# A hybrid attention/Fourier encoder layer: Nyquist weights taken from zero columns of other folds, and the rare rows of both sequences transformed together

## The chip, the cores and the metric

The kernel runs on one core of a Trainium2 chip. One launch computes a whole encoder layer for two sequences. The metric is the device time of a launch in microseconds; the median of the runs of the kernel before is 2137.72 us (2137.21 the lowest). The engines are named as in the profile: PE is TensorE (matmuls), PEld its weight loads, DVE VectorE, ACT ScalarE, POOL GpSimd, SP SyncE, which here issues most DMAs.

## The reference

Each of two sequences is x of 1024 x 1024 in fp32. The layer modulates and normalises it, projects it once, and sends the projection to two branches whose outputs are joined by one output projection; a SwiGLU FFN follows.

```python
def fourier_group(f_in, w_four):                       # f_in: (1, 1024, 512), 8 groups of 64
    f = f_in.reshape(b, s, F_GROUPS, F_GROUP_DIM).astype(jnp.float32)
    fr = jnp.real(jnp.fft.fft2(f, axes=(1, 3), norm='ortho')).astype(f_in.dtype)
    out = jnp.einsum('bsgc,gcd->bsgd', fr, w_four)
    return out.reshape(b, s, FOURIER_WIDTH)

def layer(x, c, ...):
    mod = jax.nn.silu(c) @ w_ada + b_ada
    sh1, sc1, ga1, sh2, sc2, ga2 = ...                 # six vectors of 1024
    h = rmsnorm(x, g_mix) * (1.0 + sc1) + sh1
    z = h @ w_in                                       # q_lat 256, kv_lat 128, k_pe 64, f_in 512
    y_mla = mla_group(q_lat, kv_lat, k_pe, ...)        # latent attention, 4 heads
    y_four = fourier_group(f_in, w_four)
    x = x + ga1 * (concat([y_mla, y_four]) @ w_out)
    h2 = rmsnorm(x, g_ffn) * (1.0 + sc2) + sh2
    return x + ga2 * ((silu(h2 @ w_gate) * (h2 @ w_up)) @ w_down)
```

The change touches the Fourier branch alone: a transform over the 64 channels of each group and over the 1024 positions, its real part, the per-group weights `w_four`, and the Fourier half of `w_out` scaled by `ga1`. Along the channels a real transform of 64 has 33 cosine terms (0 to 32) and 31 sine terms. The last cosine term, number 32, is the Nyquist term. It does not fit into the 32 columns that a group otherwise takes, so the kernel carries it apart: 8 groups give 8 such columns, held three times over (24 columns) for a split product.

## The kernel before, in words

**Arithmetic.** Products in full precision are made of three fast ones: `split` (L59) makes a high part with an ACT copy (L60) and a low part with a DVE subtraction (L61), and `mm3` (L70) adds high*high, high*low and low*high on PE (L71, L72, L73). The three copies of the Nyquist columns do the same inside one product: constant masks (`cmask`) pick high and low parts on both sides, so that one 24-row matmul (L702) stands for three.

**Stage 1, 0 to 246 us.** Eight pairs k = (sequence s, block j of 4) of 2 x 128 rows go through `norm` (L348, two loads of x at L354, a square sum on ACT at L356, the root on POOL in `rstd`, L95 to L102, and a scaling on DVE at L360), `flip` (L363, transposes on PE at L374 and the modulation), `zproj` (L395, the attention part of the projection, with the rotary part at L411 to L415 and the latents' scaling at L416 and L417), `latents` (L425, transposes at L431, stores to `lat_d` at L436), `evenodd` (L381, sums and differences of row halves on POOL at L390) and `fourier_in` (L438, the Fourier part). For pair k the function `pair(k)` (L507) runs the second half of pair k, the flips and even/odd parts of pair k+1 and `norm(k+2)`.

`fourier_in(k, 1)` of the pairs with j == 0 (k = 0 and k = 4) also makes `zo`, a row of the spectrum that needs the odd part of slot 0: 24 matmuls with two columns, one set for each sequence.

Between these steps a generator, `extras` (L266), is advanced three times a pair. It loads modulation weights, folds the value and output weights, and, last, folds `w_four` into `w_out`. That fold runs for two column halves g = 0, 1 (L294 to L318). Each g has four products (p = 0..3, L303) of 128 columns of `lw` with `w_out`, and a fifth group (p == 4, L306) of four matmuls with the 24 Nyquist columns, `lw[:, q, 128:152]`. A product is multiplied by the gate of each sequence on DVE (L310) into a tile `so`, which is stored by two DMAs into `wm_d` (L313); the fifth is stored by one DMA per sequence into `wn_d[s]` (L316). The tiles `so` share a ring of three buffers with other small tiles (`stile`, L168), so a new one waits until the stores of the one three places before have landed.

**Fourier stage, 246 to 350 us.** `zsplit` (L609) splits the spectrum tiles `zc`, `zs` and `zo`; `dft` (L621) does the transform over positions for q = 0, 2, 1, where q == 2 is the 24 Nyquist columns; `prep_wm` (L655) loads and splits the folded weights; `fourier_out` (L691) multiplies both and stores the result to `fo_d`, in the order j = 1, 2, 3, 0 for each sequence and for g = 0, 1. Each (j, g) has six matmuls with A, the Nyquist one (L702), and six with B; an ACT copy and two DVE operations (L127 subtracts, L130 adds) make two output tiles `ed`. For j == 0, output row 512 is added to the row that `ed[1]` holds: `dc_prep` (L676) makes the difference `dl` of two columns of A, six matmuls multiply it, L714 and L715 make two Nyquist rows, and three one-row DVE adds put them together.

**Order of the work.** The program is a plain sequence of calls; a scheduler fixes the order of instructions on each engine when the kernel is built, and engines and SP's DMA issue run in that order. An instruction that waits holds back everything behind it on its engine. Attention and FFN follow from 350 us to the end.

Of the kernel before, what the change touches and what calls it, by code (L numbers as in the profile page):

```python
# [12 lines left out]
F32 = mybir.dt.float32  # L13
# [8 lines left out]
P = 128  # L22
# [22 lines left out]
NCS = NZC + NZS  # L45
NTE = 258
# [4 lines left out]
def hybrid_encoder_kernel(ctx: ExitStack, tc: tile.TileContext, a: dict):  # L51
# [33 lines left out]
    cmask = const.tile([P, 4], F32, name="cmask")  # L85
# [28 lines left out]
    wn_d = [dram.tile([NNYQ, D], F32, name=f"wn_d{s}") for s in range(2)]  # L114
# [39 lines left out]
    zo = [zp.tile([2, NZC], F32, name=f"zo{s}") for s in range(2)]  # L154

    with ExitStack() as st:
# [23 lines left out]
        lw = w.tile([P, 4, 2 * 64 + NNYQ], F32, name="lw")  # L180
# [72 lines left out]
        def small_weights():  # L253
            w4 = w.tile([P, 4, 2, GD], F32, tag="gah0", name="w4")
            nc.sync.dma_start(w4, a["w4"])
            for b in range(2):
# [4 lines left out]
                for p in range(4):  # L261
                    o = P + 2 * p + b
                    nc.vector.tensor_copy(lw[pr, p, o : o + 17 : 8],
                                          w4[pr, p, 0, 32:33].broadcast_to([64, 3]))

        def extras():  # L266
# [27 lines left out]
            for g in range(2):  # L294
# [5 lines left out]
                for p in range(5):  # L300
                    ps = bank()
                    if p < 4:
                        nc.tensor.matmul(ps, lw[:, p, :P], wo4[p // 2][:, p % 2, gs], start=True, stop=True)  # L303
                    else:
                        for q in range(4):
                            nc.tensor.matmul(ps[:NNYQ, :], lw[:, q, P:], wo4[q // 2][:, q % 2, gs], start=(q == 0), stop=(q == 3))  # L306
                    n = P if p < 4 else NNYQ
                    for s in range(2):
                        so = stile("so")
                        nc.vector.tensor_tensor(out=so[:n], in0=ps[:n], in1=ga[s][:n], op=ALU.mult)  # L310
                        if p < 4:
                            for k in range(2):
                                nc.sync.dma_start(wm_d[s][64 * (p % 2) : 64 * (p % 2) + 64, 2 * k + p // 2, gs],  # L313
                                                  so[64 * k : 64 * k + 64, :])
                        else:
                            nc.sync.dma_start(wn_d[s][:, gs], so[:n])  # L316
                    if p % 2 == 1:
                        yield  # L318
# [119 lines left out]
        def fourier_in(k, i):  # L438
# [159 lines left out]
    with ExitStack() as st:  # L598
# [8 lines left out]
        zh, wms = {}, {}  # L607

        def zsplit(s):  # L609
            z = [[wa.tile([P, 4, n], F32R, tag=f"z{k}{i}", name=f"zh{k}{i}", bufs=1) for i in range(2)]  # L610
                 for k, n in enumerate((NZC, NZS))]
            od = [wa.tile([P, NZC], F32R, tag=f"zo{i}", name=f"zod{i}", bufs=1) for i in range(2)]
            for k, src in enumerate((zc[s], zs[s])):
                for c in range(0, 4, 2):
                    split(z[k][0][:, c : c + 2], z[k][1][:, c : c + 2], src[:, c : c + 2])
            for i in range(2):
                nc.vector.tensor_copy(od[i], rd(z[0][i][:, 0, :]))
            split(od[0][0:1, :], od[1][0:1, :], zo[s][0:1, :])
            zh[s] = (z, od)

        def dft(s):  # L621
# [3 lines left out]
            ny = w.tile([NNYQ, NT], F32R, tag="ny", name="ny", bufs=1)  # L625
            for q in (0, 2, 1):
                m = NNYQ if q == 2 else P
                sl = slice(P * q, P * q + m)
                pe, po = bank2(), bank2()
                for c in range(4):  # L630
                    mm3(pe[:m, :NTE], z[0][0][:, c, sl], z[0][1][:, c, sl], tb[0][0][:, c, :NTE], tb[0][1][:, c, :NTE],
                        c == 0, c == 3)
                for c in range(4):
                    zz = [od[i][:, sl] if c == 0 else z[0][i][:, c, sl] for i in range(2)]
# [961 lines left out]
```

## Time and profile before

| what | us |
|---|---|
| median of the runs (lowest) | 2137.72 (2137.21) |
| the profiled execution | 2136.0 |
| its span, first to last instruction | 2134.2 |
| stage 1 | 0 to 246 |
| Fourier stage | 246 to 350 |
| attention and FFN | 350 to 2134 |
| PE busy over the span | 2054.9 |
| granted TensorE clock, mean | 0.989 |

The span is what the profile shows of one execution; the device time is a little longer by what lies around the span. In the rows that are quoted below, a time in front is measured from the span's start. A row of the time line gives start, duration, engine, line, operation, output and inputs, the shape (for a matmul rows*columns of the stationary operand, then the moving one), how many instructions the row joins (x8), and in square brackets how long the engine stood idle before it and what released it. SPq rows are DMA issues of SP. Line numbers are those of the kernel before; in the changed kernel they are up to five lower in stage 1.

### The profile page before, as it was taken

The numbers are of one execution on the slowest core, as the hardware profiler recorded it, in microseconds if no ns is written. First come the engines' busy times: TensorE is split into PE (matmuls) and PEld (weight loads), VectorE is DVE, ScalarE is ACT, GpSimd is POOL, SyncE is SP. The second block draws the span as 40 slices with busy tenths as digits, with TensorE's granted clock in tenths as the row PEclk, the third lists the DMA queues.
The fourth block names the chain that finished last, engine by engine and source line by source line (L and its number), as shares of the span: only waits on it lengthen the run. The fifth ranks groups of instructions, "written<-read, shape, count | busy, mean of one in ns | idle before, by whom it ended". The sixth has DMA issues, their size and how long they took to land. (4 is left out here: it accounts for less than half of the span.)

```text
span 2134.2 us, 28930 instructions
## 1 busy us (share of the span) xinstructions
PE 2054.9 (96%) x10096; PEld 1671.4 (78%) x10096; DVE 1420.7 (67%) x2118; ACT 904.3 (42%) x1758; POOL 826.7 (39%) x1014
## 2 busy tenths in 40 slices
PE   5899998999999998999999999999999999999998
PEld 3787865888888886888888888887788888888876
DVE  2656655766676668786677667777866566557675
ACT  2655522555564546333333336444333333336441
POOL 1455202111222313797797720135545445420142
PEclk8999999999999999999999999999999999999999
DMA  9586656433545355564455468675423222248662
GB/s 366 189 248 181 225 189 234 102 92 92 138 119 124 119 182 203 187 212 168 159 206 188 153 227 290 226 237 175 148 79 119 99 101 97 99 135 290 230 226 101
DMA packets 184387, 371.11 MB, mean 174 GB/s; under 512 B 19280, under 2 KB 58832, under 8 KB 181168
## 3 DMA queue, kind: packets, MB, share of 16 engines
q1 hardware_dynamic: 166384, 313.80, 44.3%
q0 software_dynamic: 17856, 55.45, 8.8%
q8 instruction: 79, 1.29, 0.2%
q14 instruction: 68, 0.56, 0.1%
HBM read 257.18 MB, written 120.39 MB: 177 GB/s over the span
## 5 line engine op out<-in xcount | busy, mean ns | idle before, releaser
L71 PE MATMUL bank<-H,wh 128*128 128x512 f32 x1232 | 489.4, 397 | 13.5 <-DVE val L130 5.0
L73 PE MATMUL bank<-H,wl 128*128 128x512 f32 x1232 | 488.1, 396 | 1.5 <-DVE wl L61 1.5
L72 PE MATMUL bank<-H,wh 128*128 128x512 f32 x1232 | 488.2, 396 | 0.0
L130 DVE TENSOR_TENSOR val<-bank,val 128x512 f32<-128x512 f32 x244 | 167.0, 689 | 191.2 <-PE bank L73 183.4
L71 PEld LDWEIGHTS bank<-H,wh 128*128 128x128 f32 x1232 | 232.2, 188 | 73.2 <-DVE val L130 7.3
L73 PEld LDWEIGHTS bank<-H,wl 128*128 128x128 f32 x1232 | 232.0, 188 | 58.5 <-DVE wl L61 2.3
L72 PEld LDWEIGHTS bank<-H,wh 128*128 128x128 f32 x1232 | 232.0, 188 | 55.8
L61 DVE TENSOR_TENSOR wl<-draw,wh 128x512 fp32r<-128x512 f32 x286 | 200.9, 737 | 80.9 <-ACT wh L60 79.8
L60 ACT CAST wh<-draw 128x512 fp32r<-128x512 f32 x286 | 169.3, 619 | 155.3 <-PE bank L72 76.9
L72 PE MATMUL bank<-wl,wh 128*128 128x512 f32 x572 | 223.7, 391 | 2.2 <-DVE wl L61 2.2
L130 POOL TENSOR_TENSOR val<-val 128x512 f32<-128x512 f32 x58 | 82.8, 1434 | 363.5 <-DVE val L1380 188.6
L73 PE MATMUL bank<-wh,wl 128*128 128x512 f32 x572 | 222.6, 389 | 0.0
L71 PE MATMUL bank<-wh 128*128 128x512 f32 x572 | 222.6, 389 | 0.0
L60 ACT CAST wh<-rgu 128x512 fp32r<-128x512 f32 x172 | 106.7, 621 | 269.4 <-PE bank L72 211.5
L60 ACT CAST wh<-val 128x512 fp32r<-128x512 f32 x133 | 82.2, 621 | 277.6 <-PE bank L72 249.4
L61 DVE TENSOR_TENSOR wl<-val,wh 128x512 fp32r<-128x512 f32 x133 | 139.3, 1049 | 83.5 <-ACT wh L60 83.5
L61 DVE TENSOR_TENSOR wl<-rgu,wh 128x512 fp32r<-128x512 f32 x172 | 167.1, 972 | 4.8 <-ACT wh L60 4.2
L127 POOL TENSOR_TENSOR val<-rgu 128x512 f32<-128x512 f32 x84 | 122.0, 1452 | 120.3 <-DMA rgu<-in_wgu_dram 92.5
L72 PEld LDWEIGHTS bank<-wl,wh 128*128 128x128 f32 x572 | 107.3, 188 | 27.7 <-DVE wl L61 5.7
L71 PEld LDWEIGHTS bank<-wh 128*128 128x128 f32 x572 | 107.4, 188 | 22.3
L73 PEld LDWEIGHTS bank<-wh,wl 128*128 128x128 f32 x572 | 107.4, 188 | 22.1
L127 POOL TENSOR_TENSOR val<-val 128x512 f32<-128x512 f32 x89 | 119.4, 1358 | 1.3
(319 smaller groups left out, 4096.7 us busy)
## 6 DMA issues: line engine op xcount, KB each, us to landing
rgu<-in_wgu_dram SPq DMA_DIRECT2D x86, 512.0 KB, 4.2
draw<-s_d SPq DMA_DIRECT2D x143, 256.0 KB, 4.1
s_d<-val POOLq DMA_DIRECT2D x88, 256.0 KB, 4.1
draw<-t_d SPq DMA_DIRECT2D x88, 256.0 KB, 4.3
s_d<-val SPq DMA_DIRECT2D x66, 256.0 KB, 2.7
draw<-in_w_down_dram SPq DMA_DIRECT2D x55, 256.0 KB, 4.0
wada<-in_w_ada_dram SPq DMA_DIRECT2D x13, 1024.0 KB, 8.8
xt<-in_x_dram SPq DMA_DIRECT2D x16, 512.0 KB, 6.3
```

Source lines behind the costliest of these rows:

```text
L60: here["a"] = nc.scalar.copy(hi, src).ins
L61: here["v"] = nc.vector.tensor_tensor(out=lo, in0=src, in1=rd(hi), op=ALU.subtract).ins
L71: nc.tensor.matmul(out, lh, rh, start=first, stop=False, skip_group_check=cont)
L72: nc.tensor.matmul(out, lh, rl, start=False, stop=False, skip_group_check=cont)
L73: nc.tensor.matmul(out, ll, rh, start=False, stop=last, skip_group_check=cont)
L127: eng.tensor_tensor(out=out, in0=x, in1=y, op=ALU.subtract)
L130: eng.tensor_tensor(out=out, in0=x, in1=y, op=ALU.add)
```

## The change: Nyquist columns in the folds, one transform for both sequences, row 512 directly

Four things are changed.

1. *The fold.* `lw` has 128 columns instead of 152. Its columns 64 and 96 were zero, since the sine terms begin at 1; the Nyquist weights are put there, and the fifth group of matmuls (p == 4) is gone. Rows 64 and 96 of each `so` are then Nyquist rows. A third, small DMA per `so` stores these two rows three times into one `wn_d` of 48 rows for both sequences. `prep_wm` clears these rows in the folded weights with a scaling by a column of `cmask` that is 0 at every 32nd row.
2. *Slot 0.* The rows of both sequences are kept in `zoc`, and one set of 24 matmuls with four columns, in pair 4, replaces the two sets with two columns. A small DMA brings the second sequence's row to partition 0.
3. *The Nyquist transform.* `nyq_split` puts the Nyquist columns of both sequences together; `dft(0)` transforms 48 columns and `dft(1)` leaves q == 2 out. The result `ny` and the weights `wn` are padded with zeros to 128 rows, and the masks pick the sequence.
4. *Row 512.* `dc_prep` is gone. Six matmuls with columns 512:514 of A and one Nyquist matmul accumulate in one bank, and an ACT copy puts the row into `ed[1]`, in place of what stood there.

```diff
-        lw = w.tile([P, 4, 2 * 64 + NNYQ], F32, name="lw")
+        lw = w.tile([P, 4, P], F32, name="lw")
+        zoc = [w.tile([P, NC, ZOW], F32R, name=f"zoc{i}") for i in range(2)]
...
-                for p in range(4):
-                    o = P + 2 * p + b
-                    nc.vector.tensor_copy(lw[pr, p, o : o + 17 : 8],
-                                          w4[pr, p, 0, 32:33].broadcast_to([64, 3]))
+                nc.vector.tensor_copy(lw[pr, :, 64 + 32 * b], w4[pr, :, 0, 32])
...
-                for p in range(5):
+                for p in range(4):
                     ps = bank()
-                    if p < 4:
-                        nc.tensor.matmul(ps, lw[:, p, :P], wo4[p // 2][:, p % 2, gs], start=True, stop=True)
-                    else:
-                        for q in range(4):
-                            nc.tensor.matmul(ps[:NNYQ, :], lw[:, q, P:], wo4[q // 2][:, q % 2, gs], start=(q == 0), stop=(q == 3))
-                    n = P if p < 4 else NNYQ
+                    nc.tensor.matmul(ps, lw[:, p, :], wo4[p // 2][:, p % 2, gs], start=True, stop=True)
                     for s in range(2):
                         so = stile("so")
...
+                        nc.vector.tensor_tensor(out=so, in0=ps, in1=ga[s], op=ALU.mult)
+                        for k in range(2):
+                            nc.sync.dma_start(wm_d[s][64 * (p % 2) : 64 * (p % 2) + 64, 2 * k + p // 2, gs],
+                                              so[64 * k : 64 * k + 64, :])
+                        nc.sync.dma_start(
+                            wn_d[NNYQ * s : NNYQ * s + NNYQ, gs].rearrange("(k r) n -> r k n", k=3)[2 * p : 2 * p + 2],
+                            so[64:97:32, :].unsqueeze(1).broadcast_to([2, 3, 512]))
...
             if i == 1 and j == 0:
+                for k in range(2):
+                    nc.vector.tensor_copy(zoc[k][:, :, 2 * s : 2 * s + 2], rd(eo[1][k][:, :, 0:2]))
+            if i == 1 and j == 0 and s == 1:
                 po = bank()
                 for c in range(NC):
-                    mm3(po[:2, :NZC], eo[1][0][:, c, 0:2], eo[1][1][:, c, 0:2], wcs_h[:, c, :NZC], wcs_l[:, c, :NZC],
+                    mm3(po[:ZOW, :NZC], zoc[0][:, c, :], zoc[1][:, c, :], wcs_h[:, c, :NZC], wcs_l[:, c, :NZC],
                         c == 0, c == NC - 1)
-                nc.vector.tensor_copy(zo[s], po[:2, :NZC])
+                nc.vector.tensor_copy(zo[0], po[:ZOW, :NZC])
+                nc.sync.dma_start(zo[1], zo[0][2:3, :])
...
-            for q in (0, 2, 1):
-                m = NNYQ if q == 2 else P
+            for q in (0, 2, 1) if s == 0 else (0, 1):
+                m = NY2 if q == 2 else P
...
-                    split(wm[0][:, c, gs], wm[1][:, c, gs], raw)
+                    if c < 2:
+                        split(wm[0][:, c, gs], wm[1][:, c, gs], raw)
+                    else:
+                        nc.scalar.activation(wm[0][:, c, gs], raw, AF.Copy, scale=cmask[:, 6:7])
+                        nc.vector.scalar_tensor_tensor(out=wm[1][:, c, gs], in0=raw, scalar=cmask[:, 6:7],
+                                                       in1=rd(wm[0][:, c, gs]), op0=ALU.mult, op1=ALU.subtract)
...
-                wnr = w.tile([NNYQ, 512], F32, tag="wnr", name="wnr", bufs=1)
+                wnr = w.tile([P, 512], F32, tag="wnr", name="wnr", bufs=1)
+                nc.gpsimd.memset(wnr, 0.0)
+                nc.sync.dma_start(wnr[:NY2], wn_d[:, gs])
...
                 if j == 0:
-                    pn = [bank2() for _ in range(3)]
+                    pn = bank2()
                     for q in range(2):
-                        mm3(pn[0][:2, :], dl[0][:, q, :], dl[1][:, q, :], wm[0][:, q, gs], wm[1][:, q, gs], q == 0, q == 1)
-                    nc.tensor.matmul(pn[1][:2, :], ny[:, 512:514], wn[:, gs], start=True, stop=True)
-                    nc.tensor.matmul(pn[2][:2, :], ny[:, 0:2], wn[:, gs], start=True, stop=True)
-                    for q, f in enumerate((add, add, sub)):
-                        f(ed[1][0:1, :], ed[1][0:1, :], pn[q][0:1, :], nc.vector)
+                        mm3(pn[:2, :], A[0][:, q, 512:514], A[1][:, q, 512:514], wm[0][:, q, gs], wm[1][:, q, gs], q == 0, False)
+                    nc.tensor.matmul(pn[:2, :], ny[:, 512:514], wn[:, gs], start=False, stop=True)
+                    nc.scalar.copy(ed[1][0:1, :], pn[0:1, :])
```

More of the change, by code (lines that the diff above doesn't have):

```diff
@@ L45 @@
 NCS = NZC + NZS
+NY2 = 2 * NNYQ
+ZOW = 4
 NTE = 258
@@ L113, in hybrid_encoder_kernel @@
     wm_d = [dram.tile([P, 4, D], F32, name=f"wm_d{s}") for s in range(2)]
-    wn_d = [dram.tile([NNYQ, D], F32, name=f"wn_d{s}") for s in range(2)]
+    wn_d = dram.tile([NY2, D], F32, name="wn_d")
     hc_d = [dram.tile([P, 4, 4, 512], F32, name=f"hc_d{s}") for s in range(2)]
@@ L153, in hybrid_encoder_kernel @@
     zs = [zp.tile([P, 4, NZS], F32, name=f"zs{s}") for s in range(2)]
-    zo = [zp.tile([2, NZC], F32, name=f"zo{s}") for s in range(2)]
+    zo = [zp.tile([ZOW, NZC], F32, name="zo"), zp.tile([1, NZC], F32, name="zo1")]
     with ExitStack() as st:
@@ L644, in dft @@
                     nc.vector.tensor_scalar(out=al, in0=al, scalar1=cmask[:m, 1:2], scalar2=None, op0=ALU.mult)
-                    nc.vector.scalar_tensor_tensor(out=ny, in0=rd(ah), scalar=cmask[:m, 0:1], in1=al,
+                    nc.vector.scalar_tensor_tensor(out=nyt[:m], in0=rd(ah), scalar=cmask[:m, 0:1], in1=al,
                                                    op0=ALU.mult, op1=ALU.add)
@@ L689, in hybrid_encoder_kernel @@
-        dls = {}
         def fourier_out(s, ABn, j):
@@ L1539, in _constants @@
     cmask[8:16, 3] = 1
+    cmask[24:48, 0:2] = cmask[0:24, 0:2]
+    cmask[24:48, 4:6] = cmask[0:24, 2:4]
+    cmask[:, 6] = np.arange(P) % 32 != 0
     r = {
```

78 lines of the change are left out of this document (35 added, 43 removed).

## The prediction

> **What bounds the kernel now.** I read the page's head and busy times first, then a table of stages, then the order of time on single engines inside the two stages that the change touches.
>
> ```profile
> span 2134.2 us, 28930 instructions
> PE 2054.9 (96%) x10096; PEld 1671.4 (78%) x10096; DVE 1420.7 (67%) x2118; ACT 904.3 (42%) x1758; POOL 826.7 (39%) x1014
> 90.00:210.00 120.00, 119.86 (x739) 98.65 (x738) 73.89 (x148) 70.65 (x177) 62.24 (x133) 1.00 0.72 209
> 246.00:350.00 104.00, 101.08 (x504) 67.56 (x505) 67.50 (x146) 35.50 (x76) 0.00 (x0) 1.00 0.70 245
> ```
>
> Columns of the last two: stretch, its length, busy time (instructions) of PE, PEld, DVE, ACT, POOL, granted clock, DMA share, GB/s. PE is the bound: 119.86 of 120 us in most of stage 1, 101 of 104 in the Fourier stage. So PE time taken out counts in full, as long as what stands behind PE's next step in each in-order queue arrives as early as PE does. Attention and FFN, after 350, are not edited and I let them shift as a block.
>
> **PE work that goes.** Rows of PE in order of time: start, duration, line, output and inputs. Matmuls overlap, so I go from start to start.
>
> ```profile
> 85.37 0.29 PE L71 MATMUL bank<-wcs_h,eoh 128*2 128x280 f32 x1
> 88.48 0.36 PE L71 MATMUL bank<-wz_h,hh 128*128 128x448 f32 x1
> 183.86 3.61 PE L306 MATMUL bank<-wada,lw 128*24 128x512 f32 x8
> 187.41 0.47 PE L71 MATMUL bank<-wz_h,hh 128*128 128x448 f32 x1
> 208.49 1.39 PE L374 MATMUL bank<-ident,xt 128*128 128x128 f32 x8
> 209.81 3.61 PE L306 MATMUL bank<-wada,lw 128*24 128x512 f32 x8
> 213.35 0.47 PE L71 MATMUL bank<-wz_h,hh 128*128 128x448 f32 x1
> ```
>
> The 24 two-column slot-0 matmuls of the first sequence take 88.48 - 85.37 = 3.1 us; the second sequence's set stays, with 4 columns. The two Nyquist fold groups (L306) take 3.55 and 3.54. Stage 1 thus loses 10.2 us of PE work.
>
> ```profile
> 284.85 0.40 PE L73 MATMUL bank<-wm,A 128*128 128x512 f32 x1
> 285.18 0.50 PE L702 MATMUL bank<-wn,ny 24*128 24x512 f32 x1
> 285.61 0.50 PE L71 MATMUL bank<-wm,B 128*128 128x512 f32 x1
> 285.95 0.39 PE L72 MATMUL bank<-wm,B 128*128 128x512 f32 x1
> 286.18 0.40 PE L73 MATMUL bank<-wm,B 128*128 128x512 f32 x1
> 294.27 0.38 PE L715 MATMUL bank<-wn,ny 24*2 24x512 f32 x1
> 294.58 0.50 PE L71 MATMUL bank<-wm,A 128*128 128x512 f32 x1
> 304.94 0.28 PE L71 MATMUL bank<-tb,zh 128*24 128x258 f32 x1
> 307.75 0.28 PE L71 MATMUL bank<-tb,zh 128*128 128x258 f32 x1
> ```
>
> The 24-column transform of the second sequence goes: 2.8 us. A 24-row product breaks the stride: neighbours start 0.23 apart (285.95 to 286.18), but around L702 the steps are 0.33, 0.43 and 0.34, 0.40 us lost each, 16 times, 6.4 us in all. The new operands have 128 rows, zero beyond 48. The nearest row with 128 rows keeps 0.23, so I take the whole 0.40; the bounds are 0 and 6.4. In the j==0 step, two 24-row products become one of 128 rows: L715's slot goes (0.31 to the next start, 294.27 to 294.58, of which 0.08 is break), and with the smaller breaks on both sides I count 0.5, four times, 2.0 us.
>
> The Trainium skill, "TensorE: Matmul & The Clock Gate", section "Why this matters for your kernels", says that a lone matmul of few rows takes as long as one of 128; by that the padding would give nothing, 6.4 us less. The rows disagree. "TensorEngine Tiling (Array Packing)", "Key Properties", says that a change of tiling mode drains the engine; that fits the 24 rows, though the 24-column transform (304.94 to 307.75, 24 products at 0.117) shows no such drain.
>
> **End of the Fourier stage.** PE's savings do not all arrive there.
>
> ```profile
> 341.19 0.69 DVE L127 TENSOR_TENSOR ed<-ea,bank 128x512 f32<-128x512 f32 x1 [6.63 <-DMA fo_d<-ed]
> 348.75 1.44 DVE L130 TENSOR_TENSOR ed<-ed,bank 1x512 f32<-1x512 f32 x2
> 350.30 0.68 DVE L127 TENSOR_TENSOR ed<-ed,bank 1x512 f32<-1x512 f32 x1
> 349.47 0.39 PE L71 MATMUL gb<-wq_h,ql 128*128 128x256 f32 x1 [1.29 <-DVE ed L130]
> ```
>
> DVE waits 6.63 us for the stores of `ed` and is then late; PE waits 1.29 for it. Three one-row adds of about 0.67 us per (s, g) go from DVE, replaced by one ACT copy. They cover the last matmuls, so the end follows DVE's 128x512 pairs (two of 0.69 each) instead. In the second output pass PE itself would end 4.2 us earlier (8 x 0.40 + 2 x 0.5); I count 3.1, since DVE's wait for stores stays. The first pass gives 8 x 0.40 + 2 x 0.5 = 4.2, and the transform 2.8. The shared set's 48 columns cost PE nothing (a stride of 0.117 at 24 and at 128 columns), and its small splits, some 0.7 us of DVE, lie beside PE's own waits for the first splits; if not, they cost that 0.7. Fourier: 4.2 + 2.8 + 3.1 = **-10.1 us**, between -3.7 (no stride gain) and -11.2.
>
> **Stage 1: what the change moves.** Rows of SP, which issues DMAs in order, then two lines' answers: issue time in ns and time from issue to landing in us.
>
> ```profile
> 178.42 5.12 SPq L313 DMA_DIRECT2D wm_d<-so  x8
> 183.64 0.53 SPq L354 DMA_DIRECT2D xt<-in_x_dram  x1
> 197.54 5.13 SPq L313 DMA_DIRECT2D wm_d<-so  x8
> 204.12 6.44 SPq L313 DMA_DIRECT2D wm_d<-so  x8
> L316 SPq DMA_DIRECT2D wn_d<-so x4: 300/343/816, 190.2 to 216.4; - x4
> DMA to landing us min/median/max: 4.4/6.3/7.9
> ```
>
> (The last line is that of L354, the x loads.) Before, the second x load of the last pair, norm(7), is issued at 183.64, between the fold groups g=0 and g=1. In the changed program's order on SP it stands behind all of group 1: 24 `so` DMAs (three for each of eight `so`, the third new) and two latent stores. That is the costly edit, and nothing in the diff shows it. Sixteen small DMAs come, four go.
>
> The load waits for the last `so` of group 1. These come in threes of a ring, each needing its old DMAs landed. On DVE the fourth stands behind the even/odd chain of the previous pair:
>
> ```profile
> 198.53 0.60 PE L431 MATMUL bank<-ident,lat 128*128 128x128 f32 x4
> 203.44 2.99 POOL L390 TENSOR_TENSOR eo<-hf 128x512 f32<-128x512 f32 x2 [1.51 <-DVE eol L61]
> 198.58 1.05 ACT L356 ACTIVATE junk<-xt 128x1024 bf16<-128x1024 f32 x1
> 199.82 0.22 POOL L95 TENSOR_SCALAR rs_v<-ms 128x2 f32<-128x2 f32 x1 [0.93 <-ACT junk L356]
> 201.74 0.20 POOL L102 TENSOR_TENSOR rs_r<-rs_w,rs_y 128x2 f32<-128x2 f32 x1
> 203.27 0.75 DVE L360 TENSOR_SCALAR xt<-xt,rs_r 128x1024 f32<-128x1024 f32 x1
> 207.50 0.68 DVE L61 TENSOR_TENSOR eol<-eo,eoh 128x512 fp32r<-128x512 f32 x1
> ```
>
> PE is full, so the first 3.1 us carry to group 0; there the latents of pair 5 (L431) wait for a rope that now stands with the eighth `so`, which I estimate to eat most of them. So fourier_in(5,0), which ended at 198.5, ends 3.55 and a little earlier, at 194.6. The even/odd chain behind it (ACT, DVE, POOL's 2.99, ACT, DVE) took from there to 208.2 before, 9.7; I take 9.0, as DVE has fewer scalings in it now, and it ends at 203.6; the fourth `so` follows at 204. SP then needs, for five `so`, 5 x (2 x 0.64 + 0.34) = 8.1 us (0.64 from 5.12 / 8), and 1.2 for two latent stores: the load is issued at about 213.3. It lands 5.2 later (between the 4.4 and 6.3, since SP goes quiet), 218.5. Then ACT's square 1.2, POOL's chain 2.2 (199.82 to the end of 201.74), two scalings of 0.75 on DVE, the flips 0.8: zproj(6,1) starts at 224.2, where before it was 213.35. **+10.9 us.** PE, through with zproj(6,0) at about 205, has nothing ordered ahead of the flip: an idle of some 15 to 18 us.
>
> Without the chain's delay SP, kept busy from 196 on, needs 16 x 0.64 + 8 x 0.34 + 1.2 and is through at 210.2; with a landing of 4.4 that gives +7.0; with a fourth `so` 1.5 us later and a landing of 7.9, +15.0.
>
> **The clock after such an idle.**
>
> ```profile
> 78.97 1.08 PE L431 MATMUL bank<-ident,lat 128*128 128x128 f32 x4 [3.03 <-DVE lat L416]
> 80.00:81.00 1.00, 1.00 (x3) 0.48 (x2) 1.00 (x2) 1.00 (x3) 0.52 (x1) 0.50 0.23 66
> 81.00:82.00 1.00, 1.00 (x2) 0.33 (x2) 1.00 (x3) 1.00 (x3) 1.00 (x1) 0.62 0.91 263
> ```
>
> After a wait of 3.03 us the granted clock is 0.50 and recovers by 82, three us after the restart. Half of 3 us: **+1.5 us**, none at least, 1.7 at most. The Trainium skill, "TensorE: Matmul & The Clock Gate", "What's actually happening", has an idle window of about 3.4 us halve the clock until as long a busy one; the trace agrees, with the recovery at about 3.
>
> **Sum.** +10.9 + 1.5 - 10.1 = +2.3 us. The profiled execution was 2136.0 us (span 2134.2 and 1.8 around it), giving 2138.3; the median of the runs stands 1.7 above it, so **2140.0 us**, +0.1%. That is no change: about 2%, 43 us, is what a measurement of this kernel can tell.
>
> **Rivals.** *A: the load is not what PE waits for*, because the `so` queue runs ahead. Then the Fourier gain stays and stage 1 gives about -3.5 (the ring of three `so` paces group 1): 2137.7 - 13.6 = 2124.1. For it: SP has gaps between 184 and 197 now; against: SP is full at 197.54 and 204.12 as it is, and gets half as many DMAs more. *A': all PE work removed arrives*: 10.2 + 10.1, 2117.4. For it is the PE bound; against it the moved load.
>
> *B, slower: the wait is longer and the stride does not heal.* Its place is the same flip. If the last `so` comes 1.5 us later and the load takes 7.9 us, stage 1 is +15 + 1.7; if the 24-row break is of another cause than the rows (for example a first use of a new operand), Fourier is -3.7: +13.0, 2150.7. It decides once the load is issued after about 217, or if the stride around the Nyquist product stays over 0.33. Within B, no stride gain alone has 0.10 and gives +8.7, 2146.4. That is also what the Trainium skill's sentence on few rows, cited above, would make of it. *C: the change doesn't do what it says*, the folded columns costing time in later splits: `prep_wm` has the same splits, some by a scaled copy, and four clears on POOL, idle in 246 to 350; I see no more than 1 us, inside the range.
>
> **How the numbers follow.** Forecast (-6 to +8 us) 0.52; A 0.16; A' 0.07; B 0.25. The range: A's 2124.1 with 3 us under it, B's 2150.7 with 2 above: **2121 to 2153**; outside are A' and tails of B. Its sides are unlike in chance: about 0.6 for any slowing, 0.4 for any gain, but over 2%: 0.02 faster, 0.04 slower, 0.94 within.
>
> **What would show it.** In the changed profile: the second x load of the last pair at about 213 on SP, right after a run of `so` DMAs; PE's wait ahead of the flip, 15 to 18 us, in 205 to 224, released by DVE's scaling of `xt`; the clock at 0.5 in the 3 us after it; zproj(6,1) at 224; the Fourier stage starting some 12 us later than 246 and ending about 2 later than 349.47, with no step above 0.24 around the Nyquist product, now 128 rows. I am wrong if that wait is under 8 us (A), or if the Fourier stage keeps its length.

## The result: 0.28% slower, and the profile after

The changed kernel takes 2144.19 us (median), the kernel before 2138.98 over the same runs. The ratio is **1.0028, interval 1.0020 to 1.0036**: slower by about 6 us, clear of the scatter, and far inside 2%. The forecast was 2140.0, or +0.1%.

The page of the changed kernel begins so, against 2134.2 and 2054.9 before:

```profile
span 2138.3 us, 28787 instructions
PE 2036.7 (95%) x10028; PEld 1671.6 (78%) x10028; DVE 1416.3 (66%) x2087; ACT 906.5 (42%) x1763; POOL 831.4 (39%) x1018
```

PE is busy 18.2 us less, and the span is 4.1 us longer: some 22 us of new idle. The table of stretches says where (columns as in the prediction):

```profile
90.00:210.00 120.00, 113.83 (x707) 94.77 (x705) 71.22 (x140) 68.62 (x169) 59.88 (x125) 0.99 0.65 193
210.00:230.00 20.00, 4.68 (x19) 4.40 (x20) 4.16 (x10) 4.13 (x12) 4.92 (x14) 0.57 0.41 112
210.00:230.00 20.00, 20.00 (x116) 16.52 (x115) 10.77 (x20) 10.64 (x26) 9.32 (x19) 1.00 0.39 98
```

The last row is the kernel before. Between 210 and 230 us PE now works 4.68 us of 20, where before it worked 20.00 of 20. The rows in order of time show the chain, each row releasing the next (SP, then the engines ACT, POOL, DVE, PE). In the changed kernel `split` stands at L62 and L63 and the three products of `mm3` at L73 to L75:

```profile
215.75 1.09 SPq L307 DMA_DIRECT2D wm_d<-so  x2
216.88 0.54 SPq L309 DMA_DIRECT2D wn_d<-so  x1
217.52 0.34 SPq L349 DMA_DIRECT2D xt<-in_x_dram  x1
221.04 1.06 ACT L351 ACTIVATE junk<-xt 128x1024 bf16<-128x1024 f32 x1 [15.26 <-DMA xt<-in_x_dram]
222.27 0.22 POOL L97 TENSOR_SCALAR rs_v<-ms 128x2 f32<-128x2 f32 x1 [17.15 <-ACT junk L351]
224.42 1.41 DVE L355 TENSOR_SCALAR xt<-xt,rs_r 128x1024 f32<-128x1024 f32 x2 [10.01 <-POOL rs_r L104]
225.32 0.66 PE L369 MATMUL bank<-ident,xt 128*128 128x128 f32 x2 [17.17 <-DVE xt L355]
```

The second x load of the last pair is issued at 217.52, right behind the last `so` stores, where it was at 183.64 before. PE waits 17.17 us for the scaling of `xt`. Behind the wait stands a slow stretch; the granted clock is the third column from the end:

```profile
227.00:228.00 1.00, 1.00 (x5) 0.96 (x5) 0.46 (x2) 0.56 (x1) 0.75 (x4) 0.50 0.00 0
228.00:229.00 1.00, 1.00 (x5) 0.90 (x4) 0.57 (x3) 0.69 (x3) 0.23 (x1) 0.58 0.03 8
```

The Fourier stage starts 14.4 us late and makes up 9.8 of them (first rows of the stage and of attention on PE):

```profile
260.52 0.39 PE L73 MATMUL bank<-tb,zh 128*128 128x258 f32 x1 [0.98 <-ACT zh L62]
354.08 0.39 PE L73 MATMUL gb<-wq_h,ql 128*128 128x256 f32 x1 [2.73 <-DVE ed L132]
```

It takes 93.6 us instead of 103.4, and its end still waits for DVE. All stages of all kernels that follow are put side by side here; the marks are PE's start on the first transform, on the first product of attention (`gb`), on the first FFN product with `H`, and the end:

| kernel | stage 1 ends | Fourier | attention | FFN | span | ratio to before |
|---|---|---|---|---|---|---|
| before | 246.1 | 103.4 | 469.0 | 1315.7 | 2134.2 | 1 |
| before, again | 246.3 | 104.1 | 470.2 | 1315.9 | 2136.5 | |
| changed | 260.5 | 93.6 | 464.9 | 1319.4 | 2138.3 | 1.0028 |
| changed, again | 262.6 | 93.0 | 466.5 | 1321.8 | 2143.9 | |
| fold part alone | 265.5 | 103.7 | 469.3 | 1318.1 | 2156.6 | 1.0076 |
| changed without the fold part | 244.9 | 92.0 | 467.9 | 1319.5 | 2124.2 | 0.9942 |
| before, late load | 257.5 | 103.5 | 470.9 | 1318.7 | 2150.6 | 1.0051 |
| changed, early load | 250.8 | 94.2 | 465.6 | 1319.6 | 2130.2 | 0.9976 |
| changed, early load, merged store | 245.3 | 93.2 | 465.7 | 1321.2 | 2125.4 | 0.9947 |
| changed, small store by POOL | 255.8 | 94.1 | 466.0 | 1319.3 | 2135.2 | 1.0001 |
| changed, PE kept busy | 265.1 | 93.6 | 466.4 | 1316.6 | 2141.7 | 1.0010 |
| before, 128 rows | 245.4 | 98.5 | 467.7 | 1316.6 | 2128.2 | 0.9981 |
| before, row 512 direct | 244.5 | 102.6 | 463.9 | 1315.1 | 2126.2 | 0.9957 |

The first pair of profiles adds up: +14.4 - 9.8 - 4.1 + 3.6 = +4.1 us. The means of the two pairs give +15.4 - 10.5 - 3.9 + 4.8 = +5.8, close to the 5.2 between the medians.

### The profile page after: what moved, and what is told of

It is laid out like the page before. It is cut to its first block, busy times and chain, and to the rows that moved or that the text cites. A ratio compares the mean times of both kernels' runs of the same rounds, so it can differ in the third digit from the quotient of the medians.

```text
span 2138.3 us, 28787 instructions
## 1 busy us (share of the span) xinstructions
PE 2036.7 (95%) x10028; PEld 1671.6 (78%) x10028; DVE 1416.3 (66%) x2087; ACT 906.5 (42%) x1763; POOL 831.4 (39%) x1018
## 5 line engine op out<-in xcount | busy, mean ns | idle before, releaser
L73 PE MATMUL bank<-H,wh 128*128 128x512 f32 x1232 | 489.8, 398 | 15.0 <-DVE val L132 5.6
L75 PE MATMUL bank<-H,wl 128*128 128x512 f32 x1232 | 488.6, 397 | 2.0 <-DVE wl L63 2.0
L73 PEld LDWEIGHTS bank<-H,wh 128*128 128x128 f32 x1232 | 232.4, 189 | 75.2 <-DVE val L132 8.0
L75 PEld LDWEIGHTS bank<-H,wl 128*128 128x128 f32 x1232 | 232.3, 189 | 58.9 <-DVE wl L63 2.9
L63 DVE TENSOR_TENSOR wl<-draw,wh 128x512 fp32r<-128x512 f32 x286 | 202.5, 741 | 84.8 <-ACT wh L62 83.9
L62 ACT CAST wh<-draw 128x512 fp32r<-128x512 f32 x286 | 168.9, 619 | 158.1 <-PE bank L74 89.7
L75 PE MATMUL bank<-wh,wl 128*128 128x512 f32 x572 | 222.8, 390 | 0.0
L73 PE MATMUL bank<-wh 128*128 128x512 f32 x572 | 222.7, 389 | 0.0
L62 ACT CAST wh<-rgu 128x512 fp32r<-128x512 f32 x172 | 106.8, 621 | 269.7 <-PE bank L74 209.4
L62 ACT CAST wh<-val 128x512 fp32r<-128x512 f32 x133 | 82.1, 620 | 279.4 <-PE bank L74 253.9
L63 DVE TENSOR_TENSOR wl<-val,wh 128x512 fp32r<-128x512 f32 x133 | 142.4, 1072 | 83.9 <-ACT wh L62 83.8
L63 DVE TENSOR_TENSOR wl<-rgu,wh 128x512 fp32r<-128x512 f32 x172 | 167.4, 973 | 4.9 <-ACT wh L62 4.7
L73 PEld LDWEIGHTS bank<-wh 128*128 128x128 f32 x572 | 107.4, 188 | 22.4
L75 PEld LDWEIGHTS bank<-wh,wl 128*128 128x128 f32 x572 | 107.4, 188 | 21.9
```

The source lines that it names most:

```text
L62: here["a"] = nc.scalar.copy(hi, src).ins
L63: here["v"] = nc.vector.tensor_tensor(out=lo, in0=src, in1=rd(hi), op=ALU.subtract).ins
L73: nc.tensor.matmul(out, lh, rh, start=first, stop=False, skip_group_check=cont)
L75: nc.tensor.matmul(out, ll, rh, start=False, stop=last, skip_group_check=cont)
```

## Experiments

### Is it the load's place?

The first theory: what costs is that the last x load stands behind the fold's stores, and nothing else in stage 1 does. So the load is put early in the changed kernel, and late in the kernel before.

**Changed kernel, early load** (the loop body of `norm` then uses the tiles of `xload`):

```diff
+        def xload(k):
+            s, j = pairs[k]
+            xearly[k] = [xtile() for u in range(2)]
+            for u in range(2):
+                nc.sync.dma_start(xearly[k][u], xs[s][rows(j, u), :])
...
         def pair(k):
+            if k == 5:
+                xload(7)
```

> The changed kernel with one edit: the two x loads of the last pair are called at the start of pair 5, so that the second one stands on SP between the two fold groups again, as before the change, and the two scalings of xt stand before the fourth so on DVE. Theory (the moved load alone costs the 17.2 us wait): PE's wait ahead of the flip of pair 7 goes to under 3 us. What then paces stage 1 is the ring of three so, because the latents of pair 6 now stand behind the eighth so: the first transform starts 3 to 4 us earlier than in the kernel before (242 to 243 instead of 246.1), the Fourier stage stays at 93 to 94 us, and the total is about 13.5 us below the kernel before, ratio 0.9937 (0.991 to 0.995). Rival 1 (the twenty-four so DMAs themselves hold PE, wherever the load stands): the wait stays above 10 us at another line, ratio 1.000 to 1.004. Rival 2 (nothing holds PE once the load is early): all PE work removed arrives, first transform at 236, ratio 0.9905.

Ratio 0.9976 (0.9966 to 0.9987): faster than both kernels, but by 0.4 of what the theory gave. The wait ahead of the flip is gone altogether; another took part of its place (PE's and DVE's rows in order of time):

```profile
222.34 1.08 PE L435 MATMUL bank<-ident,lat 128*128 128x128 f32 x4 [5.94 <-DVE lat L420]
250.75 0.39 PE L73 MATMUL bank<-tb,zh 128*128 128x258 f32 x1 [0.98 <-ACT zh L62]
219.91 0.69 DVE L305 TENSOR_TENSOR so<-bank,gah 128x512 f32<-128x512 f32 x1 [1.09 <-DMA wn_d<-so]
221.71 0.48 DVE L420 TENSOR_SCALAR lat<-bank,rs_r 128x256 f32<-128x256 f32 x1 [1.11 <-DMA wn_d<-so]
```

The latents of pair 6 wait 5.94 us for their scaling on DVE. It stands behind the eighth `so`, and the tile `lat` takes a buffer of the same ring of three (`stile`): the eighth `so` waits 1.09 us and `lat` another 1.11 for small stores of earlier `so` to land. Stage 1 ends at 250.8, not at 242 to 243: the moved load was worth some 10 of the 14.4 us, and about 4.6 us against the kernel before stay even though 10 us of PE work are gone. The ring does pace stage 1, as the theory said, but at a much higher price than its 3 to 4 us of gain allowed for.

**Kernel before, late load:**

```diff
-                                nc.sync.dma_start(wm_d[s][64 * (p % 2) : 64 * (p % 2) + 64, 2 * k + p // 2, gs],
-                                                  so[64 * k : 64 * k + 64, :])
+                                here["so"] = nc.sync.dma_start(wm_d[s][64 * (p % 2) : 64 * (p % 2) + 64, 2 * k + p // 2, gs],
+                                                  so[64 * k : 64 * k + 64, :]).ins
...
+                    if k == 7 and u == 1:
+                        q.enter_context(tc.issue_after(here["so"]))
                     nc.sync.dma_start(t, xs[s][rows(j, u), :])
```

> The kernel before with one edit: the second x load of the last pair is ordered behind the sixteen wm_d stores of fold group 1 on SP; nothing is added or left out. Theory: the load is issued at about 210.7 (end of the stores in the kernel before), lands 3.5 to 5 us later, and square, root, scaling and flip (4.9 us) put the flip of pair 7 at 219 to 220 instead of 208.5, with the granted clock at 0.5 for some 3 us after it: the first transform starts 11 to 13 us late, ratio 1.0055 (1.005 to 1.0065). Rival (the load's place costs little, and the changed kernel waits for its third so DMA): under 3 us late, ratio under 1.0015.

Ratio 1.0051 (1.0037 to 1.0066). Only the place of one load is edited; behind it the scheduler moved some instructions around it, such as the squares, the scalings of `xt` and two fold products:

```profile
217.74 0.69 PE L377 MATMUL bank<-ident,xt 128*128 128x128 f32 x2 [8.96 <-DVE xt L363]
257.50 0.39 PE L71 MATMUL bank<-tb,zh 128*128 128x258 f32 x1 [1.02 <-ACT zh L60]
```

Stage 1 ends 11.4 us late, inside the theory's 11 to 13, though the flip came at 217.7, before the 219 to 220 that were expected. The load's place, with the order that follows from it, is shown to cost that without any third store.

### Which part of the change moves it?

**The fold part alone, on the kernel before**, and **the changed kernel without it**: both edits are the fold's hunks of the diff, once put in and once taken out.

```diff
-                for p in range(5):
+                for p in range(4):
...
+                        nc.sync.dma_start(
+                            wn_d[s][:, gs].rearrange("(k r) n -> r k n", k=3)[2 * p : 2 * p + 2],
+                            so[64:97:32, :].unsqueeze(1).broadcast_to([2, 3, 512]))
```

> The kernel before with the first part of the change alone: the Nyquist weights in columns 64 and 96 of the folds, the fifth fold group gone, three stores for each so, the rows cleared when the weights are split. The second x load of the last pair stands behind all stores of fold group 1. Theory: though 7.1 us of PE work are gone, the flip of pair 7 waits 13 to 18 us, the granted clock is at 0.5 behind it, and the first transform starts 13 to 16 us late (259 to 262); the Fourier stage is unchanged at 103.4 (a 0.5 us more or less), ratio 1.0055 to 1.0075. Rival (it needs the slot-0 part's shift of 3.1 us to bring the bad order about): first transform within 4 us of 246.1, ratio under 1.002.

> The changed kernel with its first part undone: lw has 152 columns again, the fifth fold group (L306) is back with its one store per sequence, and the third store of each so and the clearing of rows are gone; the shared transform, the shared slot 0, the 128-row operands and the direct row 512 stay. The second x load of the last pair then stands between the two fold groups on SP, as in the kernel before. Theory (the fold's part costs all that stage 1 lost): the first transform starts at 241.5 to 246 instead of 260.5, no wait of over 3 us ahead of the flip of pair 7, the Fourier stage stays at 93 to 95 us, attention as in the changed kernel, the total is 13 to 18 us below the kernel before: ratio 0.9915 to 0.994. Rival (the slot-0 part or the rest of the change moved stage 1 as well): the first transform after 248, ratio above 0.996.

The fold part alone: 1.0076 (1.0062 to 1.0090). Everything else: 0.9942 (0.9930 to 0.9954). PE's rows, first of the fold part alone, then of the rest alone:

```profile
229.70 0.66 PE L366 MATMUL bank<-ident,xt 128*128 128x128 f32 x2 [16.50 <-DVE xt L352]
265.47 0.39 PE L71 MATMUL bank<-tb,zh 128*128 128x258 f32 x1 [1.02 <-ACT zh L60]
```

```profile
244.85 0.39 PE L73 MATMUL bank<-tb,zh 128*128 128x258 f32 x1 [0.98 <-ACT zh L62]
```

The fold part removes 7.1 us of PE work and lengthens stage 1 by 19.4 us; it leaves the Fourier stage at 103.7. The rest takes 1.3 us out of stage 1 and 11.4 out of the Fourier stage. Both theories hold in kind: the first with more than its 13 to 16 us, the second with its stage 1 and its waits as expected, the Fourier stage 1 us better, and a ratio just past the edge, since its FFN took 3.8 us longer than before. The parts are not quite additive: in stage 1, 19.4 and -1.3 give 18.1, and both together measured 14.4.

### What is left when the load is early?

**Early load and merged store**: one store of 128 rows per `so` instead of two, so SP issues two DMAs for each, as before the change.

```diff
-                        for k in range(2):
-                            nc.sync.dma_start(wm_d[s][64 * (p % 2) : 64 * (p % 2) + 64, 2 * k + p // 2, gs],
-                                              so[64 * k : 64 * k + 64, :])
+                        nc.sync.dma_start(wm_d[s][:, p, gs], so)
...
-                    nc.sync.dma_start(raw, wm_d[s][:, c, gs])
+                    for b in range(2):
+                        nc.sync.dma_start(raw[64 * b : 64 * b + 64, :],
+                                          wm_d[s][64 * (c // 2) : 64 * (c // 2) + 64, 2 * (c % 2) + b, gs])
```

> The changed kernel with the early x load of the last pair, and the two wm_d stores of each so made one store of 128 rows (the load of the weights in the Fourier stage then takes two DMAs of 64 rows instead of one of 128). SP issues two DMAs for each so, as before the change, instead of three. With the early load alone, what is left of the wait is 5.94 us at the latents of pair 6 and 3.2 us at those of pair 5, where the latents' scaling stands behind so tiles that wait for their third store. Theory (SP's issue, 1.78 us for each so, paces the ring of three): the so come every 1.3 us, the 5.94 us wait goes under 2.5 us and the 3.2 us wait under 1.5, the first transform starts at 243 to 246 instead of 250.75, ratio 0.993 to 0.9955. Rival 1 (the landing of the stores, not their issue, paces the ring): the waits stay, ratio 0.997 to 0.9985. Rival 2 (the doubled loads hold up the Fourier stage): stage 1 as the theory says, but the Fourier stage is 3 us or more over its 94, ratio about 0.997.

Ratio 0.9947 (0.9933 to 0.9961). Two SP rows and two PE rows:

```profile
216.81 0.33 SPq L306 DMA_DIRECT2D wm_d<-so  x1
217.19 0.50 SPq L307 DMA_DIRECT2D wn_d<-so  x1
216.95 1.09 PE L433 MATMUL bank<-ident,lat 128*128 128x128 f32 x4 [2.95 <-DVE lat L418]
245.30 0.39 PE L73 MATMUL bank<-tb,zh 128*128 128x258 f32 x1 [0.98 <-ACT zh L62]
```

An `so` is issued in about 1.0 us instead of 1.78, the latents' wait halves from 5.94 to 2.95 (under 2.5 was expected), stage 1 ends 5.5 us earlier, and the Fourier stage does not suffer. SP's issue was a large part of what remained. The waits are 3.2 of the 5.5 us; behind them the granted clock is also higher than with the early load alone (0.79 against 0.57 in 190 to 198, and 0.76 in 216 to 223 against 0.51 in 221 to 228).

The wait at the latents of pair 5 hardly moved (3.0 instead of 3.2 us, under 1.5 was expected), so that one is not SP's issue; it is absent in the kernel without the fold part. DVE's rows show another order: first the kernel before, then this one, each time the scaling `lat` of the pair's first half and the rotary products `t` of its second half.

```profile
186.12 0.48 DVE L416 TENSOR_SCALAR lat<-bank,rs_r 128x256 f32<-128x256 f32 x1 [1.78 <-POOL rs_r L102]
193.38 0.23 DVE L411 TENSOR_TENSOR t<-bank,ropec 128x64 f32<-128x64 f32 x1 [2.61 <-ACT junk L405]
```

```profile
187.87 0.23 DVE L413 TENSOR_TENSOR t<-bank,ropec 128x64 f32<-128x64 f32 x1 [0.75 <-ACT junk L407]
188.21 0.47 DVE L418 TENSOR_SCALAR lat<-bank,rs_r 128x256 f32<-128x256 f32 x1
```

Before, the scaling stands 7 us ahead of those products; now it stands behind them, and they wait for the second half's squares on ACT. The scheduler chose this order; no run changed it alone, so its price is not shown.

**Small store by POOL:**

```diff
-                        nc.sync.dma_start(
+                        nc.gpsimd.dma_start(
                             wn_d[NNYQ * s : NNYQ * s + NNYQ, gs].rearrange("(k r) n -> r k n", k=3)[2 * p : 2 * p + 2],
```

> The changed kernel with the third, small DMA of each so issued by POOL instead of SP. SP then has sixteen issues fewer in stage 1 (0.54 us and a gap of 0.07 each), and the second x load of the last pair comes between the two fold groups by itself. Theory (SP's queue and the place of the load): the wait ahead of the flip goes, ratio 0.992 to 0.996. Rival (POOL pays: it has the even/odd sums of 1.5 us each and the roots in the same stretch, and the so ring now waits for stores that POOL issues): a wait of 4 us or more comes back at the even/odd chain or at the latents, ratio 0.997 to 1.003.

Ratio 1.0001 (0.9992 to 1.0009): the rival holds. The load is early again by itself (184.15), but the flip still waits 8.46 us, and that of the pair before waits 6.40 at 187.72, in the same way. POOL's rows, and PE's:

```profile
213.43 0.56 POOL L309 DMA_DIRECT2D wn_d<-so  x1 [3.53 <-DVE t L408]
215.38 0.22 POOL L97 TENSOR_SCALAR rs_v<-ms 128x2 f32<-128x2 f32 x1
219.81 0.69 PE L369 MATMUL bank<-ident,xt 128*128 128x128 f32 x2 [8.46 <-DVE xt L355]
```

The small store waits on POOL for a late `so`, and the root of the last pair stands behind it. The in-order wait went from one queue into another.

### The clock after the idle

**PE kept busy**: 78 products that nothing uses, ahead of the flip.

```diff
+            if k == 6:
+                warm = bank()
+                for c in range(78):
+                    nc.tensor.matmul(warm[:, :DZ], st1["hh", 6][:, c % NC, 0, :], wz_h[:, c % NC, :],
+                                     start=(c == 0), stop=(c == 77))
```

> The changed kernel with 78 extra matmuls of 128x448 ahead of the flip of pair 7, about 16 us of PE work whose result nothing uses, in the idle that lasts from 208.0 to 225.3. Theory (the idle costs a clock step on top of its length): the granted clock stays 1.00 through 225 to 229, the eight transposes and the first products of zproj(6,1) take their usual 1.0 us and 0.2 us steps, and the first transform starts 1.3 to 1.6 us earlier than in the changed kernel (259.0 instead of 260.5). Rival (the slow steps after the idle come from waits, not from the clock): no change, within 0.3 us.

Ratio 1.0010 (1.0001 to 1.0020), against 1.0028 for the changed kernel. That is 0.18% or 3.8 us less, more than the 1.5 that were expected. The profile does not show where they come from: its stage 1 is 4.6 us longer. This execution was 2.9 us late already when the load was issued, the load took 5.1 us to land instead of 3.5, and behind a later wait the clock was 0.66 in 255 to 260. So the stretch itself has to be read, from the flip to the next latents; first this kernel, then the changed one:

```profile
229.78 0.41 PE L369 MATMUL bank<-ident,xt 128*128 128x128 f32 x2 [2.52 <-DVE xt L355]
231.00:232.00 1.00, 1.00 (x8) 0.93 (x6) 0.00 (x0) 0.50 (x1) 0.72 (x4) 1.00 0.00 0
235.81 0.60 PE L426 MATMUL bank<-ident,lat 128*128 128x128 f32 x4
```

```profile
232.81 0.60 PE L426 MATMUL bank<-ident,lat 128*128 128x128 f32 x4
```

With the clock at 1.00 the stretch takes 235.81 - 229.78 = 6.03 us, without it 232.81 - 225.32 = 7.49: the clock costs **1.46 us** here. The first transform as a whole did not come 1.3 to 1.6 us earlier; that part of the expectation failed in this profile.

### The Fourier stage, by parts

**Kernel before, Nyquist operands of 128 rows:**

```diff
-            wn = w.tile([NNYQ, D], F32R, tag="wn", name="wn", bufs=1)
+            wn = w.tile([P, D], F32R, tag="wn", name="wn", bufs=1)
...
+                nc.gpsimd.memset(wnr, 0.0)
+                nc.sync.dma_start(wnr[:NNYQ], wn_d[s][:, gs])
```

> The kernel before with one edit: the Nyquist operands ny and wn have 128 rows, zero beyond the 24, so that the sixteen Nyquist products of the output passes and the eight of the j==0 steps are 128-row products. Theory (the 24 rows break PE's step): the steps around the Nyquist product go from 0.33, 0.43, 0.34 to 0.23 each; the first output pass goes from 39.5 us to 36.0 (8 x 0.40 and the two j==0 steps), the second from 32.9 to between 29.4 and 31.4, as its end waits for stores: 5.0 to 6.5 us in all, ratio 0.997. Rival (the break belongs to the product's new operand, whatever its rows): steps and passes unchanged, ratio 1.000.

Ratio 0.9981 (0.9970 to 0.9991). PE's rows around one product:

```profile
282.33 0.39 PE L73 MATMUL bank<-wm,A 128*128 128x512 f32 x1
282.56 0.40 PE L704 MATMUL bank<-wn,ny 128*128 128x512 f32 x1
282.79 0.40 PE L71 MATMUL bank<-wm,B 128*128 128x512 f32 x1
```

The steps are 0.23 and 0.23, where 24 rows gave 0.33 and 0.43. The rows of the operand are the cause, and the rival is out; why few rows break the step is not shown. The first output pass shrinks by 3.4 us (39.5 to 36.1), the second by only 1.6 (32.9 to 31.3), since its end waits for DVE and the stores.

**Kernel before, row 512 direct:** the last hunk of the diff and the removal of `dc_prep`, with the 24-row operands.

```diff
-                    for q, f in enumerate((add, add, sub)):
-                        f(ed[1][0:1, :], ed[1][0:1, :], pn[q][0:1, :], nc.vector)
+                    nc.scalar.copy(ed[1][0:1, :], pn[0:1, :])
...
-                if j == 1:
-                    dc_prep(s, abn)
```

> The kernel before with one edit: output row 512 made directly, one accumulated product and one ACT copy for each (s, g), and dc_prep, its two extra products and three one-row DVE adds gone; the Nyquist operands stay at 24 rows. Theory: the first output pass loses 2 x 0.3 us of PE (39.5 to 38.9); in the second pass DVE ends some 2.5 us earlier, and PE, which waited 1.29 us for it, starts attention 1.3 to 2 us earlier: 2 to 2.6 us in all, ratio 0.999. Rival (the end of the second pass waits for the stores of ed, and DVE's adds were hidden): second pass unchanged at 32.9, under 1 us in all.

Ratio 0.9957 (0.9942 to 0.9972), four times what was expected. The Fourier stage gains only 0.7 us in this profile: the two output passes gain 0.4 and 1.8, but the first transform takes 17.8 us instead of 16.4, at a granted clock of 0.57 (first row below). DVE's last row before attention, and PE's first row in it, which has no wait any more:

```profile
248.00:252.00 4.00, 3.99 (x20) 3.58 (x21) 3.83 (x8) 2.83 (x6) 0.00 (x0) 0.57 0.92 346
346.22 0.68 DVE L130 TENSOR_TENSOR ed<-ea,bank 128x512 f32<-128x512 f32 x1
347.16 0.39 PE L71 MATMUL gb<-wq_h,ql 128*128 128x256 f32 x1
```

The second output pass takes 31.1 instead of 32.9, and attention 463.9 instead of 469.0. In attention 4.7 of the 5.1 us come before the first product with `o1b` (first in the kernel before, 74.7 us after the start of attention, then here, 70.1):

```profile
424.22 0.40 PE L73 MATMUL gb<-wv,o1b 128*128 128x512 f32 x1
417.24 0.40 PE L73 MATMUL gb<-wv,o1b 128*128 128x512 f32 x1
```

There the order of instructions differs: without the one-row adds at the end of the pass the scheduler places the first rotary steps and scores otherwise, on PE and on DVE. The fold part alone and the 128-row kernel keep the order of before there, and need 74.6 and 73.6 us. So this small part is worth some 7 us over the last pass and attention, as much as the whole change gets there (6.6). That the order is what does it is argued, not tried: the granted clock over these 70 us differs too (0.95 here, 0.93 before, which is worth some 1.5 us).

### The same two programs again

No edit: a second profile of each, to see how far the stages of one program move.

> The changed kernel once more, for a second profile of the same program. In the first pair of profiles stage 1 took 14.4 us more, the Fourier stage 9.8 less, attention up to the first FFN product 4.2 less and the FFN, whose instructions stand in the same order, 3.7 more. Theory (attention's gain belongs to the change, since its first 70 us stand in another order; the FFN's loss is scatter from run to run): stage 1 to 260.5 within 2.5, Fourier 93.6 within 0.7, attention 464.8 within 1.5, FFN anywhere from 1315 to 1321. Rival (the FFN's loss belongs to the changed program): FFN 1319 to 1321 again, and 1314.5 to 1317 in the other kernel.

> The kernel before once more, for a second profile of the same program. Theory: first transform at 246.1 within 2.5, Fourier stage 103.4 within 0.5, attention up to the first FFN product 469.0 within 1.5, FFN anywhere from 1315 to 1321. Rival (the FFN's difference of 3.7 us belongs to the programs): FFN 1314.5 to 1317.

Stage 1, the Fourier stage and attention of the second pair lie within 2.1, 0.8 and 1.6 us of the first; the Fourier stage before (104.1) and attention after (466.5) are about 0.2 us outside what was expected. The FFN does not fit the theory of mere scatter: 1315.7 and 1315.9 before, 1319.4 and 1321.8 after, with the same order of instructions on every engine. But the changed kernel with the filler has 1316.6, and the late load on the kernel before 1318.7. PE is busy for 1291 us of the FFN in both profiles of the first pair and idle for 28.0 instead of 24.9; the extra idle is spread over waits of 0.5 to 3 us for DVE and ACT. Whether it belongs to the change stays open.

## Why the prediction was right, and where not

The direction and the mechanism held: a gain in the Fourier stage is eaten by a stall in stage 1 that a moved load makes. The size held only roughly: +2.3 us were forecast, and 5.2 lie between the medians. The 2% that the prediction took for the least that can be told was far too wide; the interval is 0.08% to each side. By its steps:

- **The moved load (+10.9).** Right in kind: the load behind the stores on SP, PE's wait of 17.2 us (15 to 18 were named), released by the scaling of `xt`. Its size was +12.3: zproj(6,1) began at 225.6 instead of 224.2. The load was issued at 217.5 instead of 213.3, for two reasons. The Fourier part of pair 5 ended at 198.0, not 194.6, because the latents of that pair waited 3.5 us (2.36 and 1.17, below) and the granted clock was 0.66 in 190 to 195, more than the "most of them" (of 3.1) that I had allowed; for that the fourth `so` came at 206.4, not 204. And from there SP took 11.1 us to the load, not 9.3: the small store was taken at the 0.34 of the 24-row store; it measured 0.54, 1.0 us over five `so`. Against that the load landed in 3.5 us instead of 5.2.

```profile
188.81 0.52 PE L426 MATMUL bank<-ident,lat 128*128 128x128 f32 x3 [2.36 <-DVE lat L411]
190.50 0.33 PE L426 MATMUL bank<-ident,lat 128*128 128x128 f32 x1 [1.17 <-POOL lat L410]
190.00:195.00 5.00, 4.50 (x14) 2.65 (x15) 2.26 (x6) 3.85 (x8) 1.67 (x5) 0.66 0.50 116
198.05 0.60 PE L426 MATMUL bank<-ident,lat 128*128 128x128 f32 x4
206.42 1.88 DVE L305 TENSOR_TENSOR so<-bank,gah 128x512 f32<-128x512 f32 x3
L309 SPq DMA_DIRECT2D wn_d<-so x16: 527/536/617, 169.3 to 216.9; - x16
```

- **The clock (+1.5).** Measured at 1.46 us for this wait. Stage 1 as a whole: +12.4 forecast, +14.4 and +16.3 in two profiles; two to four us were missing.
- **The Fourier stage (-10.1).** -9.8 and, in the second pair, -11.1. The first pass gave 4.0 (4.2 forecast), the transform of the second sequence 3.0 (2.8), the second pass 2.5 (3.1; its end still waits 2.73 us for DVE), the first transform 0.3 (0). The 24 rows were the cause of the break, as the rows said, and with 128 rows the steps around the Nyquist product are 0.23 and 0.24 in the changed kernel (293.91, 294.14, 294.38). The Trainium skill, "TensorE: Matmul & The Clock Gate", "Why this matters for your kernels", says that a single product of 32 rows takes the time of one of 128; that can't be carried over to this stream of products, in which the break is worth 0.40 us each.
- **Attention and FFN as a block (0).** This step failed. Attention took 4.1 us less; row 512 alone does as much, with another order in the first 70 us, which is the likely cause. The FFN took 3.6 us more, for a reason that is open. The two nearly cancel, so that the total came out close is partly luck.
- **Rival A (the load is not what PE waits for, -3.5 in stage 1)** is out, and its price was wrong too: with the load early, stage 1 was still 4.6 us longer than before. The ring of `so`, fed by three issues each, was a second bound that I had priced as a lost gain, not as a loss.
- **Rival B** gave +16.7 for stage 1, near the measured 14.4 to 16.3, and its sign there, a load issued after about 217, was met. Its other half, the break that stays, did not happen.

The best kernels run here are the change without its fold part (0.9942), the whole change with the early load and the merged store (0.9947), and the kernel before with row 512 direct alone (0.9957); their intervals overlap, and all three beat the kernel before and the changed one.

## What to carry to other kernels

Work taken out of the bounding engine pays only if everything that stands behind the new work in the other in-order queues still arrives in time: list, for the engine's next step, what it waits for, and look at where that now stands in each queue. Extra small DMAs are not small on the queue that issues them (0.54 us each here, beside 0.59 for a store ten times as large), and where a short ring waits for them they help to set its pace. Change parts one at a time: the fold part alone cost 0.76%, the rest gained 0.58%, and together they looked like almost nothing.

## What the runs showed of the hardware that was not expected

The same wait can cost clock in one execution and not in the next. In the two profiles of the changed kernel PE waits 2.96 and 2.98 us for the same latents near 79 us; behind it the granted clock is 0.79 in one and 1.00 in the other (first the one, then the other):

```profile
78.88 1.09 PE L426 MATMUL bank<-ident,lat 128*128 128x128 f32 x4 [2.96 <-DVE lat L411]
80.00:85.00 5.00, 5.00 (x25) 3.33 (x24) 5.00 (x8) 4.87 (x10) 1.79 (x1) 0.79 0.80 262
```

```profile
79.66 0.63 PE L426 MATMUL bank<-ident,lat 128*128 128x128 f32 x4 [2.98 <-DVE lat L411]
80.00:85.00 5.00, 5.00 (x33) 4.03 (x32) 5.00 (x9) 4.84 (x11) 1.82 (x1) 1.00 0.70 231
```

The Trainium skill, "TensorE: Matmul & The Clock Gate", "What's actually happening", says that the window in which activity is counted runs free and does not start with the kernel; these two profiles fit that. The second profile had a lower clock elsewhere (0.72 in 56 to 62 us, where the first has 1.00), and its stage 1 as a whole was 2.1 us longer. When two profiles are compared, a stretch behind a wait near 3 us may thus differ by its clock alone, whatever was changed.
